# Batched A·Bᵀ on one core: the first two loads sent whole instead of in halves, and VectorE's casts waiting for whole loads

## The chip, the cores and the metric

One core of one Trainium2 chip. The metric is the device time of one execution in microseconds (us), median of several executions; less is better. Every run told here is fast: none is over 1.5% above the fastest run of its kernel.

## The reference

```python
def setup_inputs():
    batch, m, k, n = 16, 512, 512, 512
    return {"a": randn(batch, m, k) as float32, "b": randn(batch, n, k) as float32}

def reference(a, b):
    return np.matmul(a, b.transpose(0, 2, 1)).astype(np.float32)
```

33.55 MB are read from HBM and 16.78 MB written. The kernel multiplies in bf16.

## The kernel before

SyncE loads two batches of a, then two of b, and so on: 16 loads of 2 MB, each partition with 8 rows of 2 KB, so one run of 16 KB. Seven loads have a buffer (NL = 7). The first two loads are sent as two transfers of 1 MB (runs of 8 KB), each half with its own semaphore, so that VectorE can start on the first half.

```python
def load(n):
    u, slot = n // 2, n % NL
    src = (a if n % 2 == 0 else b)[2 * u:2 * u + 2].rearrange("e (p j) k -> (e p) j k", j=2 * J)
    if n >= NL:
        nc.sync.wait_ge(s_cd, n - NL + 2)          # load n-NL+1 is being cast: the slot is free
    if n < 2:
        nc.sync.dma_start(ld[:, slot, :J, :], src[:, :J, :]).then_inc(s_ld[slot], 16)
        nc.sync.dma_start(ld[:, slot, J:, :], src[:, J:, :]).then_inc(s_second[slot], 16)
    else:
        nc.sync.dma_start(ld[:, slot], src).then_inc(s_ld[slot], 16)
```

J is 4, half of a partition's 8 rows, and HK is 256. VectorE casts each load to bf16, in columns 0 to 255 (h) and 256 to 511 (w); TensorE transposes h, VectorE then copies w over it, TensorE transposes that, and multiplies:

```python
take(s_go, 1)
# ... (a wait for TensorE, a only)
nc.vector.tensor_copy(out=h[:, :J, :], in_=src[:, :J, :HK]).then_inc(s_cd, 1)
nc.vector.tensor_copy(out=w[:, :J, :], in_=src[:, :J, HK:])
take(s_go, 1)
nc.vector.tensor_copy(out=h[:, J:, :], in_=src[:, J:, :HK]).then_inc(s_c, 1)   # h complete
nc.vector.tensor_copy(out=w[:, J:, :], in_=src[:, J:, HK:]).then_inc(s_w, 1)   # w complete
```

ScalarE brings the products out of PSUM, where TensorE leaves them, to seven output buffers. Stores 0 to 7 (1 MB each, runs of 8 KB) are issued by GpSimd, which waits with the first until the eighth load has landed; stores 8 to 15 are issued by SyncE, behind the loads.

Of the kernel before, what the change touches and what calls it, by code (L numbers as in the profile page):

```python
# [10 lines left out]
def kernel(  # L11
# [6 lines left out]
    nc = tc.nc  # L18
# [3 lines left out]
    J = M // P  # L22
    KO = K // P
    HP = P // 2
    HK = K // 2
# [3 lines left out]
    NL = 7  # L29
# [7 lines left out]
    def sbuf(name, shape, dtype):  # L37
        return ctx.enter_context(nc.sbuf_tensor(name, shape, dtype))

    def sem(name):  # L40
        return tc.alloc_semaphore(name)

    with tc.tile_critical(no_gpsimd_drain=True):  # L43
        ident = sbuf("ident", [P, P], bf16)
        one = sbuf("one", [P, 1], f32)
        ld = sbuf("ld", [P, NL, 2 * J, K], f32)
# [8 lines left out]

        s_set = sem("s_set")
        s_ld = [sem(f"s_ld{i}") for i in range(NL)]
        s_second = [sem(f"s_second{i}") for i in range(2)]
        s_st = [sem(f"s_st{i}") for i in range(batch)]

        s_go = sem("s_go")
# [19 lines left out]
            out=ident[:], in_=ident[:], compare_op=mybir.AluOpType.not_equal, fill=1.0,  # L81
# [3 lines left out]




        def load(n):
            u, slot = n // 2, n % NL  # L90
            src = (a if n % 2 == 0 else b)[2 * u:2 * u + 2].rearrange(
                "e (p j) k -> (e p) j k", j=2 * J
            )
            if n >= NL:

                nc.sync.wait_ge(s_cd, n - NL + 2)
            if n < 2:
                nc.sync.dma_start(
                    ld[:, slot, :J, :], src[:, :J, :]
                ).then_inc(s_ld[slot], 16)  # L100
                nc.sync.dma_start(
                    ld[:, slot, J:, :], src[:, J:, :]
                ).then_inc(s_second[slot], 16)
            else:
                nc.sync.dma_start(ld[:, slot], src).then_inc(s_ld[slot], 16)

        def landed(n):
            return s_st[n], 16
# [1 line left out]
        def store(n):  # L110
            engine = nc.gpsimd if n < STORES.count("S") else nc.sync
            engine.wait_ge(s_out, n + 1)
            engine.dma_start(  # L113
                out[n].rearrange("(p j) n -> p j n", j=J), ob[:, n % NO]
            ).then_inc(s_st[n], 16)

        for n in range(NL):
            load(n)
        for n in range(2 * pairs):
            got = nc.sync.wait_ge(s_ld[n % NL], 16 * (n // NL + 1))  # L120
            if n < 2:
                got.then_inc(s_go, 1)
                nc.sync.wait_ge(s_second[n], 16).then_inc(s_go, 1)
            else:
                got.then_inc(s_go, 2)

            if n > 0 and n + NL - 1 < 2 * pairs:
                load(n + NL - 1)
            for m in LATE.get(n, ()):
                store(m)  # L130
# [16 lines left out]
        def taker(engine):  # L147
            return lambda s, n: engine.wait_ge(s, n).then_inc(s, -n)  # L148
# [5 lines left out]
        take = taker(nc.vector)  # L154
# [3 lines left out]
        with nc.Fori(0, pairs, engines=[dve]) as u:  # L158
            for x, (h, w, s_c, s_w) in enumerate(
                ((ha, wa, s_ca, s_wa), (hb, wb, s_cb, s_wb))  # L160
            ):
                src = ld[:, bass.ds((u * 2 + x) % NL, 1)].rearrange("p o j k -> p (o j) k")
                take(s_go, 1)
                if x == 0:
                    take(s_da, 1)

                nc.vector.tensor_copy(  # L167
                    out=h[:, :J, :], in_=src[:, :J, :HK]
                ).then_inc(s_cd, 1)
                nc.vector.tensor_copy(out=w[:, :J, :], in_=src[:, :J, HK:])  # L170
                take(s_go, 1)
                nc.vector.tensor_copy(  # L172
                    out=h[:, J:, :], in_=src[:, J:, :HK]
                ).then_inc(s_c, 1)
                nc.vector.tensor_copy(  # L175
                    out=w[:, J:, :], in_=src[:, J:, HK:]
                ).then_inc(s_w, 1)
            for ko in range(KO):
                if ko == 0:
                    take(s_wa, 1)  # L180
                    take(s_da, 1)
                    nc.vector.tensor_copy(out=ha[:], in_=wa[:]).then_inc(s_ca, 1)  # L182
                take(s_tb, 1)
                if ko == 1:
                    take(s_wb, 1)
                    nc.vector.tensor_copy(out=hb[:], in_=wb[:]).then_inc(s_cb, 1)  # L186
                nc.vector.tensor_copy(  # L187
                    out=tb[:, ko, :],
                    in_=tp[:, 2 + ko % 2].rearrange("k j p -> k (j p)"),
                ).then_inc(s_eb, 1)  # L190
# [3 lines left out]
        take = taker(nc.scalar)  # L194
# [3 lines left out]
        with nc.Fori(0, pairs, engines=[act]) as u:  # L198
            for ko in range(KO):
# [5 lines left out]
                for e in range(2):  # L205
                    c = nc.scalar.copy(  # L206
                        out=ta[:, ko, e * J * P:(e + 1) * J * P].rearrange(
                            "k (j p h) -> k j p h", j=J, h=2
                        ),
                        in_=tp[:, ko % 2, :, e * HP:(e + 1) * HP].rearrange(  # L210
                            "k (h j) p -> k j p h", h=2
                        ),
                    )
                c.then_inc(s_ea, 1)
            for e in range(2):
                take(s_of, 1)
                dst = ob[:, bass.ds((u * 2 + e) % NO, 1)].rearrange("m o j n -> m (o j) n")
                for j in range(J):
                    if j < J - 1:
                        nc.scalar.wait_ge(s_mm, j + 1)  # L220
                    else:
# [3 lines left out]
                        out=dst[:, j, :].rearrange("m (p j) -> m p j", j=2 * J),  # L225
                        in_=ps[:, j, :].rearrange("m (j p) -> m p j", j=2 * J),
# [9 lines left out]
        take = taker(nc.tensor)  # L236
# [74 lines left out]
```

## Time and profile before

| | before |
|---|---|
| time, median of 3 runs | 125.95 us (125.94 to 126.02) |
| span in the profile | 124.2 us |
| bytes moved, mean rate over the span | 50.33 MB, 405 GB/s |
| PE (TensorE's matmuls), DVE (VectorE), ACT (ScalarE), POOL (GpSimd) busy | 74%, 56%, 55%, 5% |

Time is longer than span by 1.8 us, what lies before the first and after the last instruction. Read the profile from its slices: of 40 slices, 37 have the DMA engines at 90% or more, and the share of the busiest compute engine is 74%. The lines follow in the prediction.

### The profile page before, as it was taken

Reading aid. Unit: us, or ns where it says so; the run is one execution under the profiler, and the core shown is the slowest. Engines: PE = TensorE matmul, PEld = TensorE weight load, DVE = VectorE, ACT = ScalarE, POOL = GpSimd, SP = SyncE. Lnnn points to the kernel's source line nnn. Section 1 sums busy time; section 2 is a strip of 40 time slices with the busy share of each in tenths; the row PEclk is TensorE's granted clock in tenths of the full one; section 3 lists DMA queues with packets and bytes.
Section 4 is the critical chain, followed back from the end, with each engine's and each line's share of the span. In section 5 each row is a group of like instructions: output and inputs, shape, how many; then the busy total and the mean of one; then the engine's idle time right before and its main releaser. Section 6 shows DMA issues by size and latency. Waiting matters only on the chain. (4 is left out here: it accounts for less than half of the span.)

```text
span 124.2 us, 2416 instructions
## 1 busy us (share of the span) xinstructions
PE 92.5 (74%) x768; PEld 58.0 (47%) x768; DVE 70.0 (56%) x112; ACT 68.1 (55%) x130; POOL 6.2 (5%) x14
## 2 busy tenths in 40 slices
PE   0006299998999899899989998995699937995000
PEld 0005296467447644764575477343684426541000
DVE  0055676948992897589488578903968059400000
ACT  4005133679558946966695589435665196556000
POOL 2000000000000070002010220000000000000000
PEclk9999999999999999999999999999779999999965
DMA  4999999999999999999999999999999999999970
GB/s 84 401 425 430 443 438 428 433 428 422 428 428 428 428 438 420 401 430 430 414 425 433 430 438 417 435 435 412 454 414 433 409 430 425 430 430 425 428 327 8
DMA packets 4896, 50.33 MB, mean 405 GB/s; under 512 B 544, under 2 KB 544, under 8 KB 544
## 3 DMA queue, kind: packets, MB, share of 16 engines
q1 hardware_dynamic: 3744, 41.94, 80.2%
q0 software_dynamic: 1152, 8.39, 16.0%
HBM read 33.55 MB, written 16.78 MB: 405 GB/s over the span
## 5 line engine op out<-in xcount | busy, mean ns | idle before, releaser
L266 PE MATMUL ps<-tb,ta 128*128 128x512 bf16 x256 | 57.8, 379 | 0.4
L224 ACT COPY ob<-ps 128x512 f32 x64 | 34.4, 589 | 29.7 <-PE ps L266 26.6
L206 ACT COPY ta<-tp 128x512 bf16<-128x512 bf16 x64 | 32.9, 610 | 15.4 <-PE tp L247 15.4
L266 PEld LDWEIGHTS ps<-tb,ta 128*128 128x128 bf16 x256 | 24.2, 98 | 30.5 <-issue 3.9
L247 PE MATMUL tp<-ident,ha 128*128 128x128 bf16 x256 | 20.2, 236 | 12.6 <-PEq L148 12.6
L247 PE MATMUL tp<-ident,hb 128*128 128x128 bf16 x256 | 19.4, 236 | 8.1 <-PEq L148 7.9
L247 PEld LDWEIGHTS tp<-ident,ha 128*128 128x128 bf16 x256 | 17.5, 107 | 15.8 <-issue 14.1
L187 DVE COPY tb<-tp 128x1024 bf16<-128x1024 bf16 x32 | 21.3, 684 | 5.4 <-DVEq L148 5.3
L247 PEld LDWEIGHTS tp<-ident,hb 128*128 128x128 bf16 x256 | 17.2, 107 | 8.7 <-issue 8.7
L167 DVE CAST hb<-ld 128x1024 bf16 x8 | 5.5, 688 | 12.5 <-DVEq L148 12.3
L182 DVE COPY ha<-wa 128x2048 bf16<-128x2048 bf16 x8 | 5.5, 694 | 10.3 <-DVEq L148 10.1
L167 DVE CAST ha<-ld 128x1024 bf16 x8 | 5.5, 687 | 6.6 <-DVEq L148 6.5
L113 POOL DMA_DIRECT2D out_dram<-ob x8 | 5.5, 693 | 65.0 <-DMA ld<-in_b_dram 41.5
L172 DVE CAST hb<-ld 128x1024 bf16 x8 | 5.5, 685 | 1.1 <-DVEq L148 1.1
L172 DVE CAST ha<-ld 128x1024 bf16 x8 | 5.5, 688 | 1.0 <-DVEq L148 1.0
L186 DVE COPY hb<-wb 128x2048 bf16<-128x2048 bf16 x8 | 5.5, 685 | 0.5 <-DVEq L148 0.5
L170 DVE CAST wa<-ld 128x1024 bf16 x8 | 5.5, 686 | 0.0
L170 DVE CAST wb<-ld 128x1024 bf16 x8 | 5.5, 685 | 0.0
L175 DVE CAST wa<-ld 128x1024 bf16 x8 | 5.5, 684 | 0.0
L175 DVE CAST wb<-ld 128x1024 bf16 x8 | 5.5, 682 | 0.0
L197 ACT ACT_TABLE_LOAD x1 | 1.3, 1283 | 1.1 <-SPq L43 1.1
L80 POOL TENSOR_SCALAR_AFFINE_SELECT ident<-ident 128x128 bf16<-128x128 bf16 x1 | 0.3, 283 | 0.2 <-POOL ident L78 0.2
(6 smaller groups left out, 0.8 us busy)
## 6 DMA issues: line engine op xcount, KB each, us to landing
ld<-in_a_dram SPq DMA_DIRECT2D x7, 2048.0 KB, 29.9
ld<-in_b_dram SPq DMA_DIRECT2D x7, 2048.0 KB, 31.1
out_dram<-ob POOLq DMA_DIRECT2D x8, 1024.0 KB, 28.7
out_dram<-ob SPq DMA_DIRECT2D x8, 1024.0 KB, 20.4
ld<-in_a_dram SPq DMA_DIRECT2D x2, 1024.0 KB, 6.2
ld<-in_b_dram SPq DMA_DIRECT2D x2, 1024.0 KB, 10.2
```

Source lines behind the costliest of these rows:

```text
L113: engine.dma_start(out[n].rearrange("(p j) n -> p j n", j=J), ob[:, n % NO]).then_inc(s_st[n], 16)
L167: nc.vector.tensor_copy(out=h[:, :J, :], in_=src[:, :J, :HK]).then_inc(s_cd, 1)
L170: nc.vector.tensor_copy(out=w[:, :J, :], in_=src[:, :J, HK:])
L172: nc.vector.tensor_copy(out=h[:, J:, :], in_=src[:, J:, :HK]).then_inc(s_c, 1)
L175: nc.vector.tensor_copy(out=w[:, J:, :], in_=src[:, J:, HK:]).then_inc(s_w, 1)
L182: nc.vector.tensor_copy(out=ha[:], in_=wa[:]).then_inc(s_ca, 1)
L186: nc.vector.tensor_copy(out=hb[:], in_=wb[:]).then_inc(s_cb, 1)
L187: nc.vector.tensor_copy(out=tb[:, ko, :], in_=tp[:, 2 + ko % 2].rearrange("k j p -> k (j p)"),).then_inc(s_eb, 1)
L206: c = nc.scalar.copy(out=ta[:, ko, e * J * P:(e + 1) * J * P].rearrange("k (j p h) -> k j p h", j=J, h=2), in_=tp[:, ko % 2, :, e * HP:(e ...
L224: c = nc.scalar.copy(out=dst[:, j, :].rearrange("m (p j) -> m p j", j=2 * J), in_=ps[:, j, :].rearrange("m (j p) -> m p j", j=2 * J),)
L247: t = nc.tensor.transpose(tp[:, 2 * x + g, j, :], h[:, j, g * P:(g + 1) * P], ident[:])
L266: t = nc.tensor.matmul(ps[:, j, :], ta[:, ko, (e * J + j) * P:(e * J + j + 1) * P], tb[:, ko, :].rearrange("k (j p) -> k j p", j=2 * J)[:, ...
```

## The change

The intent is simplicity: all loads alike, one semaphore per load, one wait per load on VectorE, and one cast of 2048 elements in place of two of 1024. The price is a later start.

```diff
-            if n < 2:
-                nc.sync.dma_start(ld[:, slot, :J, :], src[:, :J, :]).then_inc(s_ld[slot], 16)
-                nc.sync.dma_start(ld[:, slot, J:, :], src[:, J:, :]).then_inc(s_second[slot], 16)
-            else:
-                nc.sync.dma_start(ld[:, slot], src).then_inc(s_ld[slot], 16)
+            nc.sync.dma_start(ld[:, slot], src).then_inc(s_ld[slot], 16)
... (SyncE signals VectorE once per load, not twice)
                 nc.vector.tensor_copy(out=h[:, :J, :], in_=src[:, :J, :HK]).then_inc(s_cd, 1)
-                nc.vector.tensor_copy(out=w[:, :J, :], in_=src[:, :J, HK:])
-                take(s_go, 1)
                 nc.vector.tensor_copy(out=h[:, J:, :], in_=src[:, J:, :HK]).then_inc(s_c, 1)
-                nc.vector.tensor_copy(out=w[:, J:, :], in_=src[:, J:, HK:]).then_inc(s_w, 1)
+                nc.vector.tensor_copy(out=w[:], in_=src[:, :, HK:]).then_inc(s_w, 1)
```

More of the change, by code (lines that the diff above doesn't have):

```diff
@@ L57 @@
         s_ld = [sem(f"s_ld{i}") for i in range(NL)]
-        s_second = [sem(f"s_second{i}") for i in range(2)]
         s_st = [sem(f"s_st{i}") for i in range(batch)]
@@ L96, in load @@
                 nc.sync.wait_ge(s_cd, n - NL + 2)
-            if n < 2:
-                nc.sync.dma_start(
-                    ld[:, slot, :J, :], src[:, :J, :]
-                ).then_inc(s_ld[slot], 16)
-                nc.sync.dma_start(
-                    ld[:, slot, J:, :], src[:, J:, :]
-                ).then_inc(s_second[slot], 16)
-            else:
-                nc.sync.dma_start(ld[:, slot], src).then_inc(s_ld[slot], 16)
+            nc.sync.dma_start(ld[:, slot], src).then_inc(s_ld[slot], 16)
         def landed(n):
@@ L119 @@
         for n in range(2 * pairs):
-            got = nc.sync.wait_ge(s_ld[n % NL], 16 * (n // NL + 1))
-            if n < 2:
-                got.then_inc(s_go, 1)
-                nc.sync.wait_ge(s_second[n], 16).then_inc(s_go, 1)
-            else:
-                got.then_inc(s_go, 2)
+            nc.sync.wait_ge(s_ld[n % NL], 16 * (n // NL + 1)).then_inc(s_go, 1)
             if n > 0 and n + NL - 1 < 2 * pairs:
@@ L174 @@
                 ).then_inc(s_c, 1)
-                nc.vector.tensor_copy(
-                    out=w[:, J:, :], in_=src[:, J:, HK:]
-                ).then_inc(s_w, 1)
+                nc.vector.tensor_copy(out=w[:], in_=src[:, :, HK:]).then_inc(s_w, 1)
             for ko in range(KO):
```

## The prediction

> **What bounds the kernel now.** I read the page's slices first, then the DMA view, then the stretches (one table of windows), then the timeline of the start and of the end, then the chain of waits and SyncE's own waits. The slices and the packet line of the page:
>
> ```profile
> DMA  4999999999999999999999999999999999999970
> GB/s 84 401 425 430 443 438 428 433 428 422 428 428 428 428 438 420 401 430 430 414 425 433 430 438 417 435 435 412 454 414 433 409 430 425 430 430 425 428 327 8
> DMA packets 4896, 50.33 MB, mean 405 GB/s; under 512 B 544, under 2 KB 544, under 8 KB 544
> ```
>
> Each slice is 3.1 us. From the second slice to the thirty-eighth the 16 DMA engines are busy without a break, at about 428 GB/s. 50.33 MB at 428 GB/s is 117.6 us of a span of 124.2 us, while PE, the busiest engine, has 92.5 us (74%). So the kernel is a DMA queue that must run dry: its time is the wait for the first byte, the ramp, the bytes, and the run-out. Rows of the table of stretches (columns: window, its length, busy us and instructions of PE, PEld, DVE, ACT, POOL, then PE's granted clock, the DMA share, GB/s):
>
> ```profile
> 2.00:4.00 2.00, 0.00 (x0) 0.00 (x0) 0.00 (x0) 0.54 (x2) 0.00 (x0) 1.00 0.93 262
> 4.00:11.00 7.00, 1.19 (x12) 1.22 (x13) 2.59 (x4) 0.14 (x1) 0.00 (x0) 1.00 1.02 428
> ...
> 22.00:32.00 10.00, 9.51 (x92) 6.13 (x91) 7.36 (x13) 7.95 (x16) 0.00 (x0) 1.00 1.00 428
> ...
> 115.00:120.00 5.00, 0.00 (x0) 0.00 (x0) 0.00 (x0) 0.00 (x0) 0.00 (x0) 0.89 1.02 429
> 120.00:121.00 1.00, 0.00 (x0) 0.00 (x0) 0.00 (x0) 0.00 (x0) 0.00 (x0) 0.50 0.34 139
> 121.00:122.00 1.00, 0.00 (x0) 0.00 (x0) 0.00 (x0) 0.00 (x0) 0.00 (x0) 0.50 0.08 33
> ```
>
> The reader is to see three things. First, the ramp: from 2 to 4 us the engines hold packets (0.93) but move only 262 GB/s, a loss of (428 - 262) x 2 us / 428 = 0.8 us. Second, the stretch that the change rewrites, 4 to 11 us, is filled by the four 1 MB half loads, with runs of 8 KB, and has 428 GB/s; the stretch 22 to 32 us, all 2 MB loads with runs of 16 KB, has the same 428. Run length is no lever here. Third, no compute engine works after 115 us, and DMA is full until 120; from 121 to 122 us the share of 0.08 is one engine of sixteen (1/16 = 0.06) that is behind the others. The sum: about 1.9 us to the first byte, 0.8 us lost in the ramp, 117.6 us of bytes, some 2 us for the engine that is behind, 1.9 us from the last byte to the end of the span: 124.2 us.
>
> The chain of waits ends in TensorE's last matmuls and the last ScalarE copy, at 113.70 + 0.58 = 114.28 us. The page names that chain last because it follows work of engines, not transfers. The last store (1 MB, 2.45 us at 428 GB/s) is queued behind others on a queue that empties at about 120.5 us, so it can't start before about 118.1 us. Issued at about 114.3 to 114.6 us, it has some 3.5 us of slack.
>
> The start, VectorE only, from the timeline:
>
> ```profile
> 6.52 0.69 DVE L167 CAST ha<-ld 128x1024 bf16 x1 [6.52 <-DVEq L148]
> 7.13 0.69 DVE L170 CAST wa<-ld 128x1024 bf16 x1
> 8.82 0.69 DVE L172 CAST ha<-ld 128x1024 bf16 x1 [1.01 <-DVEq L148]
> 9.43 0.69 DVE L175 CAST wa<-ld 128x1024 bf16 x1
> 11.38 0.69 DVE L167 CAST hb<-ld 128x1024 bf16 x1 [1.26 <-DVEq L148]
> 11.99 0.69 DVE L170 CAST wb<-ld 128x1024 bf16 x1
> 13.79 0.69 DVE L172 CAST hb<-ld 128x1024 bf16 x1 [1.12 <-DVEq L148]
> 14.40 0.69 DVE L175 CAST wb<-ld 128x1024 bf16 x1
> ```
>
> Each half load lets two casts go; the steps of 2.3 to 2.6 us between the first casts (6.52, 8.82, 11.38, 13.79) are the 2.45 us that 1 MB takes. Start to start, a cast of 1024 elements costs 0.61 us.
>
> **What the Trainium skill says.** "DMA: Bandwidth & Descriptors", section Bandwidth, measures 425 GB/s for 16 MB and derives a fabric ceiling of 435 GB/s: the 428 GB/s here is that ceiling, so only fewer bytes or less idle time at the two ends could help. The same section (Why small descriptors are slow) has the penalty in a fixed cost for a packet, large at 256 B; at 8 KB it should be invisible, and the two stretches of 428 GB/s agree. "VectorE: DVE Perf Modes", section The perf-mode tier table, gives 1227 ns for an fp32 copy of 2048 elements in SBUF. Our casts of 1024 take 686 ns; by that page the merged cast of 2048 should take about 1.2 us. No trace of before has one. "SBUF — State Buffer", section SBUF: two separate sides, warns that a VectorE copy in a two-port mode keeps GpSimd from writing descriptors for its own stores. Before, a store's issue on GpSimd takes 0.53 to 0.87 us, and DMA stays at 421 GB/s from 44 to 54 us, where four are issued: if the block occurs it is hidden by queued loads.
>
> **The change part by part.**
>
> Removed: two DMA issues (0.42 us each on SyncE's queue) and 2 x 128 data packets, with 2 x 16 that only count up the semaphore. Packets should fall from 4896 to 4896 - 256 - 32 = 4608, those under 512 B from 544 to 512. The issues cost nothing: SyncE queues 14 MB in the first 6 us, of which DMA has moved 1.5 MB by then. In the trace's packet records the median packet of 8 KB takes 309 ns and one of 16 KB 611 ns, neighbours overlapping by about 3.5 ns. On each engine 32 small packets become 16 large ones: 16 x (2 x 309 - 3.5 - 611) = 56 ns saved, and two counting packets of 5.5 ns net each. Sum: **0.07 us gained**, all on the path.
>
> Moved: the first cast waits for 2 MB instead of 1 MB. It goes from 6.52 to about 8.8 us (where the second half's cast starts now), and hb's from 11.38 to 13.8 us. But ha is only complete after the second half's cast, which starts at 8.82 now and will start at 8.8 + 0.61 = 9.4 us: **0.6 us later**. TensorE's first transposes start 0.99 us after that cast starts (9.81), so at about 10.4 us instead; those of hb at 15.4 instead of 14.78. wa follows with a cast of 1.2 us, about 1 us later than now. The first pair is thus 0.6 to 1 us late. None of it is on the path that sets the end: what DMA does in this stretch was queued by 5.74 us (seven loads); the eighth load is issued after the second has landed and its first cast is done, at 13.62 us now and about 14.5 then, with five 2 MB loads (24 us of work) still queued ahead of it. The first store waits for that eighth load, until 43 us, by GpSimd's own wait.
>
> Reordered in every pair: half h, half h, then w whole, instead of h, w, h, w. h is complete after two casts, not three: 0.6 us earlier than now after a load has landed. Two casts of 0.61 us become one of about 1.14 (start to start), so 16 x 0.08 = 1.3 us less VectorE work in all; VectorE's busy time should fall from 70.0 to 67 or 68 us, from 112 instructions to 96. It is idle 44% of the span: off the path. At the end, TensorE's last transposes may start up to 0.6 us earlier and the last store may be issued at some 113.8 us: it only waits longer in the queue.
>
> Sum: 125.95 - 0.07 = 125.88, and I say **125.9 us**.
>
> **The rivals.**
>
> 1. The late start is carried to the end: every pair follows the one before, so 0.6 to 1 us more, 126.6 to 127.0 us. For it: TensorE is busy 9.5 of 10 us from 22 to 42 us, so the lag isn't made up at once. Against it: the output of those pairs waits for GpSimd's 43 us and then for store buffers, and the last store has 3.5 us of slack.
> 2. The h that comes earlier shortens the tail: 0.6 us less, 125.3 us. For it: the page's chain ends in TensorE and ScalarE. Against it: DMA is full for more than five us after that chain has ended.
> 3. The ramp changes. The first packets took 0.35 to 1.14 us in the records instead of 0.31. If that extra is paid once per packet, whole loads with fewer packets might gain 0.2 to 0.4 us (125.5); if it goes by bytes, or if an engine that drew a bad 16 KB packet is the one that ends last, the loss is up to 0.3 us (126.2). I have nothing that decides between them.
> 4. The 1.2 us casts hold off GpSimd's descriptors longer, by up to 0.5 us for each of 8 stores. Loads hide that, but the engine that ends alone at 122.3 us may shift by a few tenths either way.
>
> **How the range and the chances follow.** Three runs of before lie within 0.08 us, so noise is small; rivals 3 and 4 each give about 0.3 us either way, rival 1 a tail above. The range is 125.5 to 126.3 us. A change of 2% is 2.5 us: more than the whole ramp, or all of the last store's wait. Faster by over 2%: 0.01; slower: 0.02; within 2%: 0.97.
>
> **What would show it right or wrong.** Right: 4608 packets; VectorE's first cast at about 8.8 us and TensorE's first transpose at about 10.4; VectorE's merged cast at about 1.2 us; DMA slices all 9 to the end and about 428 GB/s from 4 to 11 us; the last ScalarE copy ends between 113 and 115.5 us while DMA ends at 120 to 122.5. Wrong if a slice of DMA in the middle drops below 9 (a load queued too late), if the stretch from 2 to 4 us moves clearly more or less than 262 GB/s, or if the last store is issued after 118 us, which would put compute on the path.

## The result, and the profile after

The changed kernel took **125.67 us** (median of 6 runs, 125.52 to 125.93) against 125.98 us (median of 6, 125.73 to 126.06) for the kernel before. The ratio is 0.998, 95% interval 0.9964 to 0.9995. A ratio here is the mean time of one kernel's fast runs over that of the other's fast runs of the same rounds, so it isn't quite the ratio of the medians. The change is within 2%: the same, but a little faster, beyond the noise.

The page's slices and packet line after:

```profile
DMA  4999999999999998999999999999999999999980
GB/s 95 397 423 434 428 428 428 423 434 423 428 434 439 439 423 360 439 439 412 436 420 431 450 420 420 431 431 450 410 436 428 410 434 423 423 431 426 434 368 8
DMA packets 4608, 50.33 MB, mean 406 GB/s; under 512 B 512, under 2 KB 512, under 8 KB 512
```

The packets are 4608 and 512, as counted. One slice in the middle has an 8 (46.5 to 49.6 us, 360 GB/s), which the prediction had named as a sign against itself; more of it below. The stretches after, columns as before:

```profile
2.00:4.00 2.00, 0.00 (x0) 0.00 (x0) 0.00 (x0) 0.54 (x2) 0.00 (x0) 1.00 0.90 246
4.00:11.00 7.00, 0.38 (x4) 0.41 (x5) 1.97 (x3) 0.00 (x0) 0.00 (x0) 1.00 0.99 424
22.00:32.00 10.00, 9.51 (x92) 6.15 (x90) 7.07 (x11) 8.13 (x16) 0.00 (x0) 1.00 1.00 426
115.00:120.00 5.00, 0.00 (x0) 0.00 (x0) 0.00 (x0) 0.00 (x0) 0.00 (x0) 0.83 1.00 423
120.00:121.00 1.00, 0.00 (x0) 0.00 (x0) 0.00 (x0) 0.00 (x0) 0.00 (x0) 0.50 0.49 205
121.00:122.00 1.00, 0.00 (x0) 0.00 (x0) 0.00 (x0) 0.00 (x0) 0.00 (x0) 0.50 0.06 25
```

The ramp moved 246 GB/s instead of 262, the rewritten stretch 424 instead of 428: nothing gained there. The end still belongs to one engine of sixteen (0.06). VectorE's start after, from the timeline:

```profile
9.03 0.69 DVE L152 CAST ha<-ld 128x1024 bf16 x1 [9.03 <-DVEq L133]
9.64 0.69 DVE L155 CAST ha<-ld 128x1024 bf16 x1
10.24 1.22 DVE L158 CAST wa<-ld 128x2048 bf16 x1
...
13.79 0.69 DVE L152 CAST hb<-ld 128x1024 bf16 x1 [2.33 <-DVEq L133]
14.40 0.69 DVE L155 CAST hb<-ld 128x1024 bf16 x1
```

The first cast went from 6.52 to 9.03 us and the last cast of the first h from 8.82 to 9.64, so TensorE's first transpose from 9.81 to 10.62 us. A late start of 0.8 us, and a time that is 0.3 us shorter: the start isn't on the path.

**Where the 0.3 us are.** The trace also records when each of the 16 DMA engines confirms its share of a transfer. For the last store, in us from the start of the span:

```
                        the middle of the 16    second last    last
before                  120.85                  120.98         122.74
changed                 120.92                  121.28         122.52
```

In this pair of profiles the typical engine got nothing from the change. The one that ends last ended 0.22 us earlier, and the span is shorter by as much (124.17 to 123.94). The time follows that last engine: it is its confirmation plus 3.21 to 3.28 us in 13 of the 14 profiles of this document (3.46 in experiment 7). The experiments ask whether the 0.3 us come from the loads, the casts or chance, and what this late engine is.

### The profile page after: what moved, and what is told of

Read it like the earlier page. It is cut to its first block, busy times and chain, and to the rows that moved or that the text cites. A ratio compares the mean times of both kernels' runs of the same rounds, so it can differ in the third digit from the quotient of the medians.

```text
span 123.9 us, 2364 instructions
## 1 busy us (share of the span) xinstructions
PE 91.9 (74%) x768; PEld 56.9 (46%) x768; DVE 68.5 (55%) x96; ACT 68.0 (55%) x130; POOL 5.5 (4%) x14
## 2 busy tenths in 40 slices
DMA packets 4608, 50.33 MB, mean 406 GB/s; under 512 B 512, under 2 KB 512, under 8 KB 512
## 5 line engine op out<-in xcount | busy, mean ns | idle before, releaser
L228 PEld LDWEIGHTS tp<-ident,ha 128*128 128x128 bf16 x256 | 17.0, 105 | 17.9 <-issue 16.0
L228 PE MATMUL tp<-ident,hb 128*128 128x128 bf16 x256 | 18.8, 232 | 6.7 <-PEq L133 6.7
L228 PEld LDWEIGHTS tp<-ident,hb 128*128 128x128 bf16 x256 | 16.6, 105 | 7.2 <-issue 7.2
L158 DVE CAST wa<-ld 128x2048 bf16 x8 | 9.8, 1220 | 0.0
L158 DVE CAST wb<-ld 128x2048 bf16 x8 | 9.8, 1219 | 0.0
L103 POOL DMA_DIRECT2D out_dram<-ob x8 | 4.8, 607 | 65.5 <-DMA ld<-in_b_dram 41.5
## 6 DMA issues: line engine op xcount, KB each, us to landing
out_dram<-ob POOLq DMA_DIRECT2D x8, 1024.0 KB, 29.2
```

The costliest lines, as they stand in the source:

```text
L103: engine.dma_start(out[n].rearrange("(p j) n -> p j n", j=J), ob[:, n % NO]).then_inc(s_st[n], 16)
L158: nc.vector.tensor_copy(out=w[:], in_=src[:, :, HK:]).then_inc(s_w, 1)
L228: t = nc.tensor.transpose(tp[:, 2 * x + g, j, :], h[:, j, g * P:(g + 1) * P], ident[:])
```

## The experiments

Twelve runs, each in rounds with the kernel before on the same chip. Where a table says "last minus middle", it is the lateness of the last engine at the last store in the one profiled run, as above. The trace doesn't number the engines, so that the late one is the same from run to run is assumed.

**1. Again, and again.** The changed kernel, unaltered.

> The changed kernel again, unaltered, as the yardstick of this call. Theory (a full DMA queue sets the end, and the change saves packets and a little of the engine that runs behind): 0.1 to 0.35 us below the kernel before, ratio 0.997 to 0.999. Rival (the 0.2% of the first comparison was chance): ratio 0.9995 to 1.001. Packets 4608, the last transfer of the engine that runs behind lands 1.2 to 1.7 us after the second last engine.

> The changed kernel once more, on the same chip as the run above, as its yardstick: 125.5 to 125.9, ratio to before 0.9965 to 0.999.

Measured: 125.63 us against 125.90, ratio 0.997 (0.9955 to 0.9985), and 125.55 us against 125.91, ratio 0.9969 (0.995 to 0.9988). With the first comparison that makes three, each with an interval below 1. The gain of some 0.3 us isn't chance.

**2. The casts alone.** Loads in halves, casts in the new order:

```diff
  # the kernel before, with
-                nc.vector.tensor_copy(out=w[:, :J, :], in_=src[:, :J, HK:])
                 take(s_go, 1)
                 nc.vector.tensor_copy(out=h[:, J:, :], in_=src[:, J:, :HK]).then_inc(s_c, 1)
-                nc.vector.tensor_copy(out=w[:, J:, :], in_=src[:, J:, HK:]).then_inc(s_w, 1)
+                nc.vector.tensor_copy(out=w[:], in_=src[:, :, HK:]).then_inc(s_w, 1)
```

> Only the casts of the change (half h, half h, then w whole); the first two loads stay in halves, and h's second cast still waits for the second half. Theory that the gain is in the transfers: as the kernel before within 0.1 us, ratio 0.999 to 1.001, packets 4896. Rival that the gain comes from the casts (h complete 0.6 us sooner in every pair, or fewer and longer VectorE copies beside GpSimd's stores): ratio 0.997 to 0.9985, like the changed kernel.

Measured: 125.95 us, ratio 1.000 (0.9986 to 1.0014). With the loads in halves the new casts give nothing, though h is complete 0.6 us sooner in every pair.

**3. The whole loads alone.** The changed kernel with the casts in four pieces, in the old order:

```diff
  # the changed kernel, with
+                nc.vector.tensor_copy(out=w[:, :J, :], in_=src[:, :J, HK:])
                 nc.vector.tensor_copy(out=h[:, J:, :], in_=src[:, J:, :HK]).then_inc(s_c, 1)
-                nc.vector.tensor_copy(out=w[:], in_=src[:, :, HK:]).then_inc(s_w, 1)
+                nc.vector.tensor_copy(out=w[:, J:, :], in_=src[:, J:, HK:]).then_inc(s_w, 1)
```

> Only the whole loads of the change; the casts in the old order h, w, h, w in four pieces. Theory that the gain is in the transfers: 0.1 to 0.35 us below the kernel before, ratio 0.997 to 0.999, packets 4608, although ha is complete only some 1.2 us later than before (about 10.7 us, TensorE's first transpose at about 11.2 us). Rival that the gain comes from the casts: ratio 0.9995 to 1.001. Rival that a late start is carried to the end: 0.6 to 1.2 us above the kernel before, ratio 1.005 to 1.01.

> Whole loads with the old order of casts once more, because its first result (ratio 0.9996, interval 0.998 to 1.0012) fell between the two readings. If the whole loads alone carry the gain: ratio 0.997 to 0.9985. If the gain needs the new casts too: 0.9992 to 1.0005. In between, it stays unresolved: the whole effect is 0.3 us.

Measured: 125.85 us, ratio 0.9996 (0.998 to 1.0012); then 125.63 us, ratio 0.9988 (0.9974 to 1.0002). The first ratio lies in the rival's band (0.9995 to 1.001), the second between the two readings, and both intervals include 1. The first runs of experiments 1, 2 and 3 shared their rounds and their chip, so their means can be put side by side:

| mean of the runs, us | old casts | new casts |
|---|---|---|
| loads in halves | 125.94 | 125.98 |
| loads whole | 125.86 | 125.59 |

There the whole loads with the old casts are 0.27 us slower than the changed kernel; from the spread of the runs that is uncertain by some 0.16. The repeat, on another chip and without the changed kernel beside it, was 0.19 us below the kernel before. So whole loads alone are worth 0.1 to 0.2 us, not clear of zero, the new casts alone nothing, and both together 0.35. Why the parts don't add up isn't shown.

**4. A start that is late by five microseconds.** VectorE's loop begins only when the second load has landed too:

```diff
         nc.vector.wait_ge(s_set, 2)
+        nc.vector.wait_ge(s_ld[1], 16)
```

> The changed kernel, but VectorE's first cast waits for the second load too: at about 13.8 instead of 9.0 us, a start later by 4.8 us, eight times what the change itself cost. Theory (seven loads queued, the end set by DMA): time of the changed kernel within 0.15 us, ratio to before 0.997 to 0.9995; the last ScalarE copy may end up to 1 us later. Rival 1 of the prediction (a late start is carried to the end): 4 to 5 us slower, ratio 1.03 to 1.04.

Measured: 125.71 us, ratio 0.9982 (0.9968 to 0.9996): as the changed kernel. The first cast and the last row of ScalarE's timeline (two copies, so it ends at 114.70 us; 113.92 in the changed kernel):

```profile
14.27 0.69 DVE L153 CAST ha<-ld 128x1024 bf16 x1 [14.27 <-DVEq L133]
```

```profile
113.61 1.09 ACT L206 COPY ob<-ps 128x512 f32 x2 [0.60 <-PE ps L248]
```

Of 5.2 us at the start, 0.8 are left at ScalarE's end and nothing in the time. Rival 1 of the prediction is refuted for delays of this size.

**5. The slack at the end.** SyncE releases the last load to VectorE only after store 9 has landed (stores 12 and 13 are issued before that, so that the queue isn't starved of them):

```diff
         for n in range(2 * pairs):
+            if n == 2 * pairs - 1:
+                store(batch - 4)
+                store(batch - 3)
+                nc.sync.wait_ge(*landed(9))
             nc.sync.wait_ge(s_ld[n % NL], 16 * (n // NL + 1)).then_inc(s_go, 1)
... (stores 12 and 13 taken out of their later place)
```

> The changed kernel, but SyncE lets VectorE take the last load only after store 9 has landed (107.6 us in the changed kernel), instead of at 100.0 us: the last pair comes some 7.5 us later. It measures the slack at the end. Theory: the last two stores have 2.8 to 3.5 us of wait in the queue, so the delay shows up as 7.5 - 2.8 = 4.7 us for most DMA engines, and some 3.5 to 4.7 us in the time: 129.2 to 130.4 us, with DMA slices that fall below 9 near 116 to 120 us. Rival that the end was set by the chain in TensorE and ScalarE, as the page's chain could be read: all 7.5 us, 133 us. Rival that the slack is larger than I think: under 2 us.

Measured: 129.31 us, ratio 1.0277 (1.0261 to 1.0293). The last ScalarE copies and the stretches:

```profile
120.68 1.09 ACT L209 COPY ob<-ps 128x512 f32 x2 [0.60 <-PE ps L251]
```

```profile
112.00:116.00 4.00, 4.00 (x30) 2.76 (x29) 1.59 (x3) 2.07 (x5) 0.00 (x0) 0.78 0.85 358
116.00:118.00 2.00, 2.00 (x11) 0.88 (x9) 0.00 (x0) 1.41 (x4) 0.00 (x0) 1.00 0.01 4
118.00:120.00 2.00, 2.00 (x11) 0.92 (x10) 0.00 (x0) 1.31 (x3) 0.00 (x0) 1.00 0.00 0
```

ScalarE's end moved from 113.92 to 121.77 us, by 7.85 us, and the time by 3.7 us (129.3 - 125.6). By this one delay the slack of the time is 7.85 - 3.7 = 4.1 us; the prediction had some 3.5. It is the late engine's: the middle engine confirms the last store at 125.90 us, 5.0 later than in the changed kernel, so its slack was only 2.9. Past that the queue runs dry, as the rows show, and all 16 engines confirm the last store within 0.2 us: the late engine had caught up.

**6. Runs of 8 KB everywhere.** All 16 loads in two transfers, VectorE waiting for both:

```diff
-            nc.sync.dma_start(ld[:, slot], src).then_inc(s_ld[slot], 16)
+            nc.sync.dma_start(ld[:, slot, :J, :], src[:, :J, :]).then_inc(s_ld[slot], 16)
+            nc.sync.dma_start(ld[:, slot, J:, :], src[:, J:, :]).then_inc(s_ld[slot], 16)
... (32 per load in the waits on s_ld, 64 in GpSimd's)
```

> The changed kernel with every one of the 16 loads sent as two transfers in runs of 8 KB, VectorE waiting for both: the cost of the shorter run by itself, sixteen times 2 MB instead of two. By the packet times (309 ns against 611 ns) 16 loads x 33.5 ns = 0.54 us above the changed kernel, so about 0.2 us above the kernel before, ratio to before 1.001 to 1.003; packets 6656. Rival that run length costs nothing and the gain was the first packets' ramp: as the kernel before (it shares its first 4 MB), ratio 0.9995 to 1.0005. Rival that stores get a larger share of the engines while smaller load packets alternate with 8 KB store packets: loads then land later from 45 us on, and the time could go either way by 0.5 us.

Measured: 127.29 us, ratio 1.0115 (1.0096 to 1.0133): 1.7 us above the changed kernel, more than any of the three readings and three times the estimate for the packets (the packet count in the expectation is wrong as well: it is 6912, since each half adds its own 16 counting packets). The rows of DMA issues of the changed kernel and of this one (transfers, KB each, median us from issue to landing), then the cast of the last load and a stretch of this one:

```profile
out_dram<-ob POOLq DMA_DIRECT2D x8, 1024.0 KB, 29.2
```

```profile
out_dram<-ob POOLq DMA_DIRECT2D x8, 1024.0 KB, 19.3
```

```profile
103.75 0.69 DVE L153 CAST hb<-ld 128x1024 bf16 x1 [1.01 <-DVEq L134]
```

```profile
115.00:118.00 3.00, 3.00 (x15) 1.18 (x12) 0.00 (x0) 1.71 (x4) 0.00 (x0) 1.00 0.61 257
```

The stores took 19.3 us instead of 29.2 to land, and the last load's cast began at 103.75 us instead of 100.08. The landings show the sharing. Between 55 and 98 us the changed kernel lands 2 MB of loads and 1 MB of stores every 7.3 us; this one lands 1 MB of each every 4.9 us. With load packets cut to half, the loads' part of the bytes falls from two thirds to one half. ScalarE's end came at 118.83 us, 4.9 later than in the changed kernel, so the slack was gone, and DMA lost (1 - 0.61) x 3 us = 1.2 us between 115 and 118 us. How the 1.7 us divide isn't settled: the middle engine ended 2.0 us later than in the changed kernel, the last one 1.4, since it still had work while the others were dry, and the packets cost more than the estimate (experiment 7).

**7. Only the loads that share with no store.** The first seven loads in halves (all landed before the first store is issued at 43 us), the rest whole.

```diff
+            if n < NL:   # two transfers of 1 MB, as in the run before
+                ...
+            else:
                 nc.sync.dma_start(ld[:, slot], src).then_inc(s_ld[slot], 16)
... (the waits on s_ld count accordingly)
```

> The changed kernel with the first seven loads (all that land before the first store is issued at 43 us) in two transfers of 8 KB runs each, the other nine whole. All loads in halves cost 1.66 us more than the changed kernel, three times the 0.54 us of the packets. Theory: the rest came from sharing, since a load packet of 8 KB alternates with a store packet of 8 KB and the loads then get half of the engines, not two thirds, so that the last load came 3.7 us later and the queue ran dry at the end. Here no halved load shares with a store, so only the packets are left: 7 x 33.5 ns = 0.23 us above the changed kernel, minus or plus the ramp's 0.2: 125.7 to 126.1 us, ratio to before 0.999 to 1.0015; last load's first cast at 100 to 100.5 us. Rival that halves cost three times what I think: 7/16 of 1.66 = 0.7 us above the changed kernel, ratio about 1.003 to 1.005.

Measured: 126.62 us, ratio 1.0059 (1.0047 to 1.0072), above what either reading expected. Part of that is outside the span: time minus span is 2.01 to 2.09 us in this kernel's six runs and 1.76 to 1.87 in all other runs, 0.25 us whose cause I don't know. (VectorE starts only at 13.96 us here, and at 14.09 in experiment 6, since SyncE issues all its transfers before it looks at the first load; experiment 4 shows such a delay to be free.) The mean span is 124.5 us, against 123.8 for the changed kernel: 0.7 us for seven loads, or **0.1 us for each halved load**, where the estimate has 0.033 us.

The estimate is too low already for the typical engine. From the landing of the second load (13 us) to that of the eighth (42 us), the middle engine takes 29.36 to 29.38 us in all ten profiles with whole loads, 29.74 here, where five of these six loads are halved, and 29.83 in experiment 6, where all six are: 0.075 us for each. The estimate used median packets; between 13.5 and 42 us the mean packet takes 313 ns in experiment 6 and 613 in the changed kernel, which by the prediction's sum makes 0.086 us. Against it stands the start: the second load lands at 13.02 to 13.08 us in the four profiles whose first loads are halved, at 13.11 to 13.27 in the ten others. At the end the middle engine is 0.03 us later than in the changed kernel, and the last one, at 122.93 us, 0.41 later.

The profiles of experiments 1 to 4 and of this one side by side, at the last store:

| kernel (first two loads) | middle engine | last engine | last minus middle |
|---|---|---|---|
| before (halves) | 120.85 | 122.74 | 1.89 |
| new casts (halves) | 120.88 | 122.87 | 2.00 |
| seven loads in halves | 120.95 | 122.93 | 1.98 |
| changed, three profiles (whole) | 120.92, 120.83, 120.72 | 122.52, 122.43, 122.43 | 1.60, 1.60, 1.71 |
| old casts, two profiles (whole) | 120.85, 120.80 | 122.46, 122.33 | 1.60, 1.53 |
| late start (whole) | 120.82 | 122.57 | 1.75 |

Three profiles with halves have 1.89 to 2.00, six with whole loads 1.53 to 1.75: in these profiles the late engine is some 0.3 us less late with whole loads. But a profile is one run, and the cut of the loads doesn't settle it. At the store before the last, where the profiles of experiments 8 to 10 can be compared too, the halves have 1.85 to 1.96, eight profiles with whole loads 1.48 to 1.71, and experiment 9, with whole loads, 1.83.

Nor is the lateness there at the start. When the eighth load lands, the last engine is 0.47 or 0.48 us after the middle with halves and 0.27 to 0.59 with whole loads. The difference arises between 47 and 99 us, while loads and stores share the engines. By 99 us the three profiles with halves, and experiment 9, have a last load whose last engine is 1.5 to 1.7 us behind the middle, and a store landing beside it with only 0.4 to 0.5; in the other profiles with whole loads both have 0.76 to 1.15. What sends the late engine into the one pattern or the other is not shown.

**8. Is the late engine GpSimd's doing?** Stores 0 to 7 issued from ScalarE's queue, at about the same moments; ScalarE's loop is written out for that:

```diff
-            engine = nc.gpsimd if n < STORES.count("S") else nc.sync
+            engine = nc.scalar if n < 8 else nc.sync
... (in ScalarE's program, pair 2: wait for the eighth load, store(0) to store(3); pair 3: wait
     landed(0), store(4); then landed(1), store(5); pair 4: landed(2), store(6), store(7))
```

> The changed kernel with its first eight stores issued from ScalarE's queue instead of GpSimd's, at about the same moments (four at 43 us, the fifth after the first has landed, and so on); GpSimd only counts landings. It tests what makes one DMA engine run behind between 48 and 106 us. If it is GpSimd's software queue: that engine ends with the others, within 0.5 us instead of 1.2 to 1.7, and the time falls by about 1.0 to 1.4 us, to 124.2 to 124.8, ratio to before 0.987 to 0.991. Rival that it is the stores themselves, or that engine, whatever the queue: same gap, time within 0.2 us of the changed kernel, ratio 0.997 to 0.999. Rival that ScalarE's issues (some 0.4 us each) hold up its copies and the path: slower; I expect no more than 3 us of ScalarE time, all of it before the tail.

Measured: 125.76 us, ratio 0.999 (0.9976 to 1.0003). The queues of this run:

```profile
q1 hardware_dynamic: 3456, 41.94, 80.4%
q10 hardware_dynamic: 1152, 8.39, 16.0%
```

A third row, two packets of instructions, is left out. No transfer goes through the software queue, and the late engine is as late: 122.49 us, 1.61 after the middle. My favoured reading, a gain of 1.0 to 1.4 us, was wrong: the software queue doesn't cause it.

**9. Which engine is it?** The last store cut by partitions, so that the highest-numbered engine has no part in it:

```diff
+            cuts = ((0, 120), (120, P)) if n == batch - 1 else ((0, P),)
+            for lo, hi in cuts:
+                engine.dma_start(dst[lo:hi], ob[lo:hi, n % NO]).then_inc(s_st[n], 16)
... (the wait for this store counts 32)
```

> The changed kernel with its last store cut by partitions: 120 of them in a transfer that 15 DMA engines share, the last 8 in a transfer on 8 engines, so that the highest-numbered engine has no part in the last 1 MB (2.45 us less work) and eight others one packet more (0.31 us). It asks which engine runs behind at the end. If it is that one: it ends before the others, the last transfer lands at 121.2 to 121.7 instead of 122.5 us, time 124.5 to 125.1, ratio to before 0.989 to 0.994. If it is another: one engine ends 2.4 us early, the late one is as late as before or 0.3 us later; time 125.6 to 126.1, ratio 0.997 to 1.001.

The numbering is the rule of the Trainium skill, "DMA: Bandwidth & Descriptors", section Why a DMA increments its semaphore by 16 and not by 1: a transfer over k engines, issued as here by SyncE, goes to the k lowest-numbered of the core. The count of confirmations agrees with 15 and 8 engines; which ones they are no run here shows. Measured: 126.23 us, ratio 1.0029 (1.0011 to 1.0047), slower, and above both bands: some 0.6 us above the changed kernel, where one packet explains 0.3. In this profile the late engine was later than usual already before the last store (1.83, above). The packets of the late engine show it directly: it counts up for the large part, moves one packet more (309 ns), counts up again, and lands at 122.67 and 122.97 us. So it is one of the eight engines that took the small part.

**10. The eighth of them?** Three cuts, so that by the same rule engine 7 has two packets less and engines 0 to 6 have three more:

```diff
+            cuts = ((0, 80), (80, 115), (115, P)) if n == batch - 1 else ((0, P),)
... (the wait for this store counts 48)
```

> The changed kernel with its last store cut into 80 partitions for all 16 DMA engines (five each), 35 for the first seven (five each) and 13 for the first thirteen (one each). The run before showed that the engine that ends late is one of the first eight. By this cut the eighth of them has 6 packets of the last store instead of 8, the first seven have 11. If the late engine is the eighth (number 7): it ends 2 x 0.31 us earlier, at about 121.9 us, and the first seven, which have some 1.3 us in hand, at about 121.8: time 124.9 to 125.3, 0.4 to 0.6 us below the changed kernel, ratio to before 0.992 to 0.996. If it is one of the first seven: 3 x 0.31 = 0.9 us later, 126.4 to 126.8, ratio 1.003 to 1.007.

Measured: 126.63 us, ratio 1.0058 (1.004 to 1.0076); the last confirmation at 123.23 us. The end of this run in stretches:

```profile
121.00:122.00 1.00, 0.00 (x0) 0.00 (x0) 0.00 (x0) 0.00 (x0) 0.00 (x0) 0.50 0.12 49
122.00:123.00 1.00, 0.00 (x0) 0.00 (x0) 0.00 (x0) 0.00 (x0) 0.00 (x0) 0.50 0.04 16
```

It is 1.1 us slower than the changed kernel in the same rounds (125.55, the second repeat of experiment 1); three packets more are 0.93 us. If the rule of numbering holds, the late engine of this run is one of 0 to 6. No run tells which. I found no version that beats the changed kernel.

## Why the prediction was right or wrong

- **The bound** was right. DMA is full from 3 to 120 us in both kernels; 5.2 us at the start changed nothing, and at the end some 4.1 us of delay were free.
- **The removed packets**: their number was right (4608 and 512), but the step "0.07 us gained, all on the path" failed twice. For the typical engine the term is too small and not alone: a halved load costs 0.075 us in a full queue (experiment 7), which the two windows of 428 GB/s were too coarse to show, so "run length is no lever" was wrong as well. Yet whole loads start more slowly, and the middle engine landed the eighth load at 42.48 to 42.64 us with whole loads, against 42.43 in both kernels with two halves: about 0.1 us later, not 0.07 earlier. And the path isn't the typical engine's. It runs through the last engine, and the time fell by some 0.3 us, four times the term. The prediction had seen this engine (share 0.08 from 121 to 122 us) and treated its lateness as a constant; in the table of experiment 7 it is anything from 1.53 to 2.00 us.
- **The moved start**: hb's transposes at 15.38 us (15.4 predicted) and the eighth load's issue at 14.51 us (14.5) were met. ha's came at 10.62 us (10.4): the first load's last engine confirmed at 8.60 us and the cast began at 9.03, not 8.8.
- **The casts**: the merged cast took 1.22 us, as the page on VectorE led me to expect. VectorE's busy time fell to 68.5 us, not to 67 or 68 (the prediction's own saving of 1.3 us gives 68.7); nothing hangs on it. Experiment 2 shows that the reordering alone gives no time; beside whole loads it may (experiment 3).
- **Rival 1** is refuted (experiment 4), **rival 2** too: ScalarE ended at 113.92 instead of 114.28 us, but experiment 5 shows that this end has some 4 us of slack, and experiment 2, which has the same casts, gained nothing.
- **Rival 3**: fewer packets did not shorten the ramp. From 2 to 4 us, profiles with halves move 258 to 270 GB/s; those with whole loads spread from 221 to 270; the changed kernel's 246 against 262 is the sign that the prediction had named. The first 16 packets of 8 KB took 0.35 to 1.14 us in the kernel before, the first 16 of 16 KB 0.61 to 1.76 in the changed one, and the second load landed about 0.1 us later. Of the two readings, the loss was nearer.
- **Rival 4** was not seen: GpSimd's issues became shorter (mean 607 ns after 693), and experiment 8 shows that an engine is as late without its queue. (The prediction's window of 44 to 54 us has three of the first four issues, which run from 43.2 to 45.9 us.)
- **The sign that fired falsely**: the slice with an 8 at 46.5 us isn't a load queued too late. In the packet records the engines are busy there for 0.999 of the time, if packets are cut at the slice's edges; between 45 and 48 us, just after the first four stores start, some 30 load packets take 40 to 400 ns more than their 611. The kernel before has such packets too, spread over 46 to 62 us, and halves with new casts has 388 GB/s in that slice.
- **The range**, 125.5 to 126.3 us, held, and 125.9 was 0.2 too high. That no change over 2% came was reasoned; that the small gain had the predicted sign was luck, since the saving named for it isn't where the gain came from.

## What to carry to other kernels

When a queue of transfers is full from start to end, an earlier start of compute buys nothing, and the care spent on it (half loads, extra semaphores) can go. Before shortening anything, measure the slack by a deliberate delay: here 5 us at the start and 4 us at the end were free. And look at the last DMA engine, not at the mean of sixteen: it alone sets the end, and the size of load packets beside store packets decides how the two share (two thirds of the bytes for loads of 16 KB beside stores of 8 KB, one half for 8 KB).

## What the Trainium skill lacked or had wrong

- "DMA: Bandwidth & Descriptors", section Latency and other measured facts, says that DMA engines 7 and 15 are usually the slower ones and guesses that this belongs to GpSimd's software queue. Here one engine ends 1.5 to 2.0 us after the middle of the others; it does so without the software queue too (1.61 us), and by the page's own rule of numbering it is one of 0 to 6 in the run that tests it (the cut that relieves engine 7 ended at 123.23 us).
- The same page has packet cost as a matter of small runs. Here cutting runs of 16 KB to 8 KB costs 0.075 us per 2 MB load on the middle engine while the queue is full (1.5% of 4.9 us), and 0.1 us of span in the kernel with seven loads cut; no page has this.
- The same page, section Queues, rings and completion order, says that an engine goes round between queues packet by packet, and the shares of loads and stores here (2 to 1 with packets of 16 and 8 KB, 1 to 1 with 8 and 8) agree. It doesn't draw the consequence: halving the load packets shortened stores from 29.2 to 19.3 us and delayed the last load by 3.7 us, in a kernel that took 1.7 us longer.
- No page has the cold start of a queue: the first 16 packets take 0.35 to 1.14 us instead of 0.31 (8 KB, before) and 0.61 to 1.76 instead of 0.61 (16 KB, after), and from 2 to 4 us 221 to 270 GB/s are moved instead of 428.
